# Sparse layer of a four-layer encoder: q, k and v of the first eight heads in steps of 512 columns over four banks

## The chip, the cores and the metric

The kernel runs on one core of one Trainium2 chip. The metric is the device time of one execution in microseconds (us). Engines: PE is TensorE (matmuls), DVE is VectorE, ACT is ScalarE, POOL is GpSimd, SP issues the loads of weights.

## What is computed

Four residual layers, `x <- x + Mixer(RMSNorm(x))`, on 512 tokens of width 1024: a gated short convolution (layer a), sparse attention (layer b), latent attention (layer c), and layer a once more. The change is in layer b:

```python
def dsa_mixer(xn, positions, w_in, q_norm, k_norm, w_out):
    q, k, v, z, qi, ki, wi = jnp.split(xn @ w_in, cuts, axis=-1)
    q = rope(rmsnorm(q.reshape(bsz, seq, B_HEADS, B_HEAD_DIM), q_norm), positions)
    k = rope(rmsnorm(k.reshape(bsz, seq, B_HEADS, B_HEAD_DIM), k_norm), positions)
    ...
        rel = jax.nn.relu(jnp.einsum("qhd,sd->qhs", qi_b, ki_b).astype(jnp.float32))
        score = jnp.einsum("qh,qhs->qs", w_b.astype(jnp.float32), rel)
        ...
        top_val, top_idx = lax.top_k(score, topk)
        ...
        logits = jnp.einsum("qhd,qkhd->qhk", q_b, k_sel).astype(jnp.float32) * scale
    ...
    return (o * jax.nn.silu(z)) @ w_out
```

There are 16 heads of 64, a gate `z` of 1024 columns, and an indexer (`qi`, `ki`, `wi`) whose scores choose 128 keys for each query. Layer b's input projection has 4680 columns.

## The kernel before

Each product of float32 matrices is made of three matmuls, of high and low halves: `products` (lines 277 to 282) multiplies high by high, high by low and low by high into the same PSUM bank. Activations are split once a layer into `xh`, `xl`. Weights come as `raw` tiles of 512 KB from the SP queue, in the order that `enter` (1084 to 1089) writes down, three tiles ahead. `convert` (141 to 163) makes a unit of 512 columns of them: ACT writes the high half `whi` (line 155), POOL the low half `wlo` (line 157). A unit is four rows of eight in a gate block of 128 columns, two in a group of 256 columns, one in a group of 512. Up to three units are made ahead, in rings of four.

Layer b projects first the indexer, then six of its eight gate blocks (`gate_steps`, 712: tile `pz`, 24 matmuls of 512 columns each) and, for heads 0 to 3 (group 0) and 4 to 7 (group 1), q, k and v. `tokens` (311) has the activations of 128 tokens as the stationary side and the weights as the moving one: a group of 256 columns takes 8 x 4 x 3 = 96 matmuls of 256 columns into two banks, each bank holding two blocks of tokens. `project` (866) takes the banks in turn from `pj` and `pt`, two of each. Its finish `fin` (823) runs per bank: ACT copies and squares it (825, 827), DVE sums the squares by head (828), POOL multiplies by the cosine table (`ropea`, line 551), DVE reads the bank twice more for the sine part (`ropeb`, 555), POOL adds (558). Then POOL makes the reciprocal root of the 16 sums per token (`small_rsqrt`, 269, line 274), scales (842 to 851), and `to_features` (563) turns the result with four PE transposes per pair of heads (`tr`), which ACT copies (571) and DVE splits (572).

Beside this `select` (777) makes the index scores: per block of 128 tokens four groups of six matmuls (`si`, line 288), eight `rel` tiles that DVE adds up (792, 794), and 16 rounds of MAX8 and MATCH_REPLACE8 on DVE (799, 800), then a mask (803). Blocks 1, 2 and 3 have 256, 384 and 512 columns; the third mask is `mask3`. `weave` runs the two side by side in the program; the engines' final order is set by a scheduler that works with its own model of times.

`attention` (603) then goes through eight pairs of heads, four blocks of tokens each. The scores of a pair (`s`, line 288) lie in one double bank; DVE adds the mask (638), ACT takes the exponential, DVE the factor `rc` (651), POOL or ACT scales (656, 658), PE turns the probabilities (`pt`, 668). Between these steps a filler runs the projections of groups 2 and 3 (here: late q, k and v), with 256 columns as before and after the change.

Of the kernel before, what the change touches and what calls it, by code (L numbers as in the profile page):

```python
# [10 lines left out]
F32 = mybir.dt.float32  # L11
# [3 lines left out]
OP = mybir.AluOpType  # L15
# [56 lines left out]
def encoder(ctx: ExitStack, tc: tile.TileContext, a, out, depth=4):  # L72
# [6 lines left out]
    def const(shape, name, dtype=F32):  # L79
        return sb.tile(shape, dtype, name=name, bufs=1)  # L80
# [6 lines left out]
    def tile_of(tag, name, shape=(P, S), dtype=F32):  # L87
        return sb.tile(list(shape), dtype, name=name, tag=tag, bufs=BUFS[tag])
# [2 lines left out]
        return tile_of("rp", name, shape, dtype)  # L91

    def tiny(name, n, dtype=F32, tag="tiny"):
        return sb.tile([P, n], dtype, name=name, tag=tag, bufs=24)

    def bank(name, tag):
        return ps.tile([P, S], F32, name=name, tag=tag, bufs=BANKS[tag])
# [132 lines left out]
    def chain(*gens):  # L230
        for g in gens:
            yield from g
# [30 lines left out]
            y = z  # L263
        return y

    minus_half = const([P, 16], "minus_half")
    pool.memset(minus_half, -0.5)

    def small_rsqrt(v, n, scale, out=None):

        m = tiny("mean", n)
# [66 lines left out]
    def by_head(x):  # L338
        return x.rearrange("p (t h) -> p t h", h=4)
# [394 lines left out]
    def layer_b(last):  # L734
# [74 lines left out]
        def token_factors():  # L809

            for name, k in (("r2", None), ("rs", -B_SCALE)):
# [3 lines left out]
                else:  # L815
                    pool.tensor_scalar(st[name], st["r"], k, 0.0, op0=OP.mult, op1=OP.add)


        def query_key(group, which, scales, dst, banks):
            raw = []  # L820
            sums = tiny("hs", 16)

            def fin(i, b):
                x = tile_of("qk", "qk", (P, 2, 256))
                act_e.activation(x.rearrange("p t c -> p (t c)"), b, AF.Copy)
                q = tile_of("rp", "qk2", (P, 2, 256))
# [4 lines left out]
                x5, b5 = (y.rearrange("p t (h i j) -> p t h i j", h=4, i=2)  # L831
                          for y in (x, b.rearrange("p (t c) -> p t c", c=256)))
                C, T = (tab[:, 2 * i:2 * i + 2] for tab in (tq if which == "q" else tk))
                rotate(x5, x5, C, T, b5)

            yield from tokens(group, act, fin, banks)
            v = tiny("hv", 16)
            pool.tensor_tensor(out=by_head(v), in0=by_head(sums), in1=st["r2"][:, :, None].to_broadcast([P, NT, 4]),
                               op=OP.mult)
            y = small_rsqrt(v, 16, 1.0 / 64)  # L840
            if which == "q":
                pool.tensor_tensor(out=scales, in0=by_head(y), in1=st["rs"][:, :, None].to_broadcast([P, NT, 4]),
                                   op=OP.mult)
            else:
                f = tiny("hf", 16)
                pool.tensor_tensor(out=by_head(f), in0=by_head(y), in1=st["r"][:, :, None].to_broadcast([P, NT, 4]),
                                   op=OP.mult)
            for i, x in enumerate(raw):
                if which == "k":
                    x3 = x.rearrange("p t (h d) -> p (t h) d", d=64)  # L850
                    pool.tensor_tensor(out=x3, in0=x3, in1=f[:, 8 * i:8 * i + 8, None].to_broadcast([P, 8, 64]),
                                       op=OP.mult)

            for p in range(2):
                to_features(dst[p], lambda t: raw[t // 2][:, t % 2, p * P:(p + 1) * P], P)

        def values(group, dst, banks):
            def fin(i, b):
                for j in range(2):
                    t = 2 * i + j  # L860
                    act_e.activation(dst[i][:, j], b[:, j * 256:(j + 1) * 256], AF.Copy, scale=st["r"][:, t:t + 1])
            yield from tokens(group, act, fin, banks)

        sets = {}

        def project(g, tags):
            s = sets[g] = dict(qs=sb.tile([P, NT, 4], F32, name="qs", tag="qs", bufs=2))
            for n, w in enumerate("qkv"):
                banks = [bank("p" + w, tags[n % len(tags)]) for _ in range(2)]
                group = a["b_" + w][g]  # L870
                if w == "v":
                    s[w] = [tile_of("v", "v", (P, 2, 256)) for _ in range(2)]
                    yield from values(group, s["v"], banks)
                else:
                    s[w] = [[tile_of("T", w + "T", dtype=F32R) for _ in range(2)] for _ in range(2)]
                    yield from query_key(group, w, s["qs"], s[w], banks)

        def job(pair, after, fill):
            g, i = divmod(pair, 2)

            def scores(outs, t):
# [17 lines left out]
        attention([job(p, p // 2 - 2, ends[p:p + 2]) for p in range(8)],  # L899
                  Filler([project(g, ["pj"]) for g in range(2, 4)] + [gate_steps(a["b_z"][6:], R, gate)]))  # L900
        branch_out(a["b_out"], gate, last)


# [217 lines left out]
def pack(inputs):  # L1121
# [74 lines left out]
```

## Time and profile before

| | us |
|---|---|
| median of three runs | 1062.6 (1060.54 to 1065.26) |
| the profiled execution's own time | 1062.74 |
| its span | 1060.9 |
| PE busy | 1043.6 |
| POOL busy | 694.1 |
| DVE busy | 531.2 |
| ACT busy | 511.2 |

The profile is of one execution; the times in it run from the start of its span. Busy time of an engine is the time in which at least one instruction is on it; matmuls overlap, so PE's busy time says little about how fast they follow one another, for which one looks at their starts. Idle time is shown with what ended it. The first gate block of layer b starts at 254.1 us, layer c at 569.0.

### The profile page before, as it was taken

What the parts mean: (1) busy time and instruction counts of PE and PEld (TensorE: products, weight loads), DVE (VectorE), ACT (ScalarE), POOL (GpSimd) and SP (SyncE); (2) the same over time, 40 slices, a digit from 0 to 9 for tenths busy, and PEclk for the clock granted to TensorE, in tenths of its full rate; (3) what the DMA queues carried; (4) which work ended last, traced back from release to release, by engine and by line L of the source; (5) the groups of instructions that cost most, each with busy time, mean ns of one, the idle gap of its engine ahead of it and who ended that gap; (6) DMA issues with size and microseconds to landing.
All of it is one profiled execution on the core that took longest, in us unless ns stands there. A gap on an engine that the chain in (4) does not pass through costs nothing.

```text
span 1060.9 us, 16208 instructions
## 1 busy us (share of the span) xinstructions
PE 1043.6 (98%) x6040; PEld 877.3 (83%) x6040; DVE 531.2 (50%) x1064; ACT 511.2 (48%) x1082; POOL 694.1 (65%) x637
## 2 busy tenths in 40 slices
PE   8999999999999999999999999999999999999998
PEld 7888888898798999998788777787878888888887
DVE  6784334435598984343535233444542764344321
ACT  6243323433444457666744437876773533333231
POOL 6656555666469799686548689788743855555552
PEclk9999999999999999999999999999999999999999
DMA  6333333323222131111122221101211333333332
GB/s 207 106 114 88 95 97 100 92 69 110 80 80 80 61 99 41 61 61 54 48 70 77 81 74 50 41 23 61 80 40 40 100 99 99 99 100 99 99 100 80
DMA packets 26574, 86.43 MB, mean 81 GB/s; under 512 B 3328, under 2 KB 4096, under 8 KB 26496
## 3 DMA queue, kind: packets, MB, share of 16 engines
q1 hardware_dynamic: 26352, 85.36, 25.6%
q8 instruction: 47, 0.77, 0.3%
q14 instruction: 31, 0.25, 0.1%
q10 hardware_dynamic: 144, 0.05, 0.0%
HBM read 83.30 MB, written 2.10 MB: 80 GB/s over the span
## 4 chain that ended last, share of the span: by engine, by line
PE 91%; POOL 3%; ACT 2%; DVE 2%; issue 1%; DMA 1%; SPq 0%; POOLq 0%; ACTq 0%; DVEq 0%
PE pa L281 11%; PE pa L279 10%; PE pa L280 10%; PE po L279 6%; PE po L280 6%; PE po L281 5%; PE o L689 3%; PE pt L668 3%; PE s L1062 3%; PE pz L281 2%; PE pz L279 2%; PE pz L280 2%; PE s L288 2%; PE tr L568 2%; PE pq L279 2%; PE pk L280 1%
## 5 line engine op out<-in xcount | busy, mean ns | idle before, releaser
L157 POOL TENSOR_TENSOR wlo<-raw,whi 128x512 fp32r<-128x512 f32 (+4 forms) x316 | 408.6, 1300 | 260.3 <-ACT whi L155 256.1
L155 ACT ACTIVATE whi<-raw 128x512 fp32r<-128x512 f32 (+3 forms) x320 | 195.5, 615 | 334.6 <-PE pa L280 157.5
L280 PE MATMUL pa<-xl,whi 128*128 128x512 f32 x512 | 199.4, 389 | 1.1 <-DVE xl L358 1.1
L279 PE MATMUL pa<-xh,whi 128*128 128x512 f32 x512 | 198.9, 390 | 0.2 <-ACT xh L357 0.2
L281 PE MATMUL pa<-xh,wlo 128*128 128x512 f32 x512 | 198.1, 389 | 0.4 <-POOL wlo L157 0.4
L280 PEld LDWEIGHTS pa<-xl,whi 128*128 128x128 f32 x512 | 96.1, 188 | 21.8 <-DVE xl L358 1.7
L279 PEld LDWEIGHTS pa<-xh,whi 128*128 128x128 f32 x512 | 96.3, 188 | 20.6 <-ACT xh L357 0.8
L281 PEld LDWEIGHTS pa<-xh,wlo 128*128 128x128 f32 x512 | 96.0, 188 | 20.9 <-POOL wlo L157 0.9
L656 POOL TENSOR_SCALAR p<-p,rc 128x128 f32<-128x128 f32 (+1 forms) x64 | 69.3, 1088 | 45.5 <-DVE rc L651 45.2
L641 ACT ACTIVATE p<-p,mn 128x128 f32<-128x128 f32 (+3 forms) x128 | 71.0, 557 | 16.5 <-DVE mn L638 16.4
L463 DVE TENSOR_TENSOR cg<-pa,R 128x512 f32<-128x512 f32 x16 | 11.0, 690 | 123.4 <-PE pa L281 121.1
L638 DVE CUSTOM_DVE_ANT_0 p<-s,cmask,qs 128x128 f32<-128x128 f32 (+2 forms) x80 | 37.8, 505 | 35.2 <-PE s L1062 21.2
L281 PE MATMUL pz<-xh,wlo 128*128 128x512 f32 x128 | 51.3, 403 | 0.1
L279 PE MATMUL pz<-xh,whi 128*128 128x512 f32 x128 | 50.9, 398 | 0.2 <-ACT whi L155 0.2
L673 ACT ACTIVATE p<-pt 128x384 f32<-128x384 f32 (+1 forms) x80 | 39.1, 507 | 24.8 <-PE pt L668 24.6
L280 PE MATMUL pz<-xl,whi 128*128 128x512 f32 x128 | 50.4, 394 | 0.0
L280 PE MATMUL po<-xl,whi 128*128 128x512 f32 x128 | 50.3, 393 | 0.0
L668 PE MATMUL pt<-ident,p 128*128 128x128 f32 x320 | 49.2, 277 | 1.0 <-ACT p L673 0.7
L274 POOL TENSOR_TENSOR y<-mean,minus_half 128x16 f32<-128x16 f32 (+1 forms) x18 | 49.6, 2757 | 0.7
L280 PE MATMUL po<-glo,whi 128*128 128x512 f32 x128 | 49.8, 389 | 0.0
L279 PE MATMUL po<-xh,whi 128*128 128x512 f32 x128 | 49.5, 398 | 0.0
L279 PE MATMUL po<-ghi,whi 128*128 128x512 f32 x128 | 49.5, 389 | 0.0
(244 smaller groups left out, 2432.4 us busy)
## 6 DMA issues: line engine op xcount, KB each, us to landing
raw<-in_a_in SPq DMA_DIRECT2D x63, 512.0 KB, 3.9
raw<-in_a_out SPq DMA_DIRECT2D x16, 512.0 KB, 3.9
raw<-in_b_z SPq DMA_DIRECT2D x8, 512.0 KB, 3.5
raw<-in_b_q SPq DMA_DIRECT2D x8, 512.0 KB, 3.5
raw<-in_b_k SPq DMA_DIRECT2D x8, 512.0 KB, 3.5
raw<-in_b_v SPq DMA_DIRECT2D x8, 512.0 KB, 3.5
raw<-in_b_out SPq DMA_DIRECT2D x8, 512.0 KB, 3.9
raw<-in_c_z SPq DMA_DIRECT2D x8, 512.0 KB, 3.5
```

The lines of the kernel that those rows point to most:

```text
L155: act_e.activation(hi[:, :, :n], raw[:, j:j + m], AF.Copy)
L157: e.tensor_tensor(out=lo, in0=raw[:, j:j + m, :n - few], in1=hi[:, :, :n - few].bitcast(F32), op=OP.subtract)
L274: pool.tensor_tensor(out=y, in0=m, in1=minus_half[:, :n], op=OP.pow)
L279: nc.tensor.matmul(o, l[0], r[0], start=first, stop=False)
L280: nc.tensor.matmul(o, l[0], r[1], start=False, stop=False)
L281: nc.tensor.matmul(o, l[1], r[0], start=False, stop=last)
L638: dve.tensor_tensor_reduce(out=p[:, w], in0=banks[e][:, w], in1=j["masks"](t), scale=j["qs"](e, t), scalar=-GONE, op0=OP.add, op1=OP.min, ...
L641: act_e.activation(p[:, w], p[:, w], AF.Exp, bias=mn[e][:, i:i + 1], scale=-1.0, accum_out=sm[:, e * n + i:e * n + i + 1])
L656: pool.tensor_scalar(p[:, w], p[:, w], rc[:, i:i + 1], None, op0=OP.mult)
L668: pe.transpose(b[:, i:i + P], p[:, i:i + P], ident)
L673: act_e.activation(p[:, :n], b[:, :n], AF.Copy)
L689: pe.matmul(o[64 * e:64 * e + 64, t * P:(t + 1) * P], j["v"](e, kb), x[e][:, i:i + P], start=first, stop=t == 0)
```

## The change

The weights of q, k and v for heads 0 to 7 are stored as one group of 512 columns each. `tokens` takes such a group with 8 x 4 x 3 = 96 matmuls of 512 columns into four banks, one block of tokens in each; the four are the two of `pj` and the two of `pt`, for q, for k and for v alike. The early part of layer b becomes: gate blocks 0, 1, 2, q, gate block 3, k, gate block 4, v, gate block 5. Blocks 3 to 5 use the bank `o`, so the transposes from there on have only `tr`. One reciprocal root covers 32 columns in place of two of 16, in place. The ring of small tiles has 20 buffers for 24. Groups 2 and 3 are as they were.

```diff
-    minus_half = const([P, 16], "minus_half")
+    minus_half = const([P, 32], "minus_half")
...
         def query_key(group, which, scales, dst, banks):
+
+            heads = group.n // 64
+            per = NT // len(banks)
             raw = []
-            sums = tiny("hs", 16)
+            sums = sb.tile([P, NT * heads], F32, name="hs", tag=f"hs{heads}", bufs=2)
 
             def fin(i, b):
-                x = tile_of("qk", "qk", (P, 2, 256))
+                x = tile_of("qk", "qk", (P, per, group.n))
                 act_e.activation(x.rearrange("p t c -> p (t c)"), b, AF.Copy)
...
             yield from tokens(group, act, fin, banks)
...
+            y = by_token(sums, heads)
+            pool.tensor_tensor(out=y, in0=y, in1=st["r2"][:, :, None].to_broadcast([P, NT, heads]), op=OP.mult)
+            small_rsqrt(sums, NT * heads, 1.0 / 64, sums)
...
-            for p in range(2):
-                to_features(dst[p], lambda t: raw[t // 2][:, t % 2, p * P:(p + 1) * P], P)
+            for p, x in enumerate(dst):
+                to_features(x, lambda t: raw[t // per][:, t % per, p * P:(p + 1) * P], P)
...
+        def only_tr():
+            early_turns[0] = False
+            yield from ()
...
-        early = chain(gate_steps(a["b_z"][:4], R, gate, "pj"), project(0, ["pj", "pt"]),
-                      gate_steps(a["b_z"][4:6], R, gate, "pj"), project(1, ["pj", "pt"]))
+        def four(name):
+            return lambda: [bank(name, tag) for tag in ("pj", "pj", "pt", "pt")]
+
+        early = chain(gate_steps(a["b_z"][:3], R, gate, "pj"), only_tr(),
+                      *(x for i, which in enumerate("qkv") for x in
+                        (project(which, [0, 1], four("p" + which)), gate_steps(a["b_z"][3 + i:4 + i], R, gate, "o"))))
...
-            enter(a["b_idx"] + a["b_z"][:4])
-            for g in range(4):
+            enter(a["b_idx"] + a["b_z"][:3])
+            for i, w in enumerate("qkv"):
+                enter([a["b_" + w][0], a["b_z"][3 + i]])
+            for g in range(1, 3):
                 enter([a["b_" + w][g] for w in "qkv"])
-                if g == 0:
-                    enter(a["b_z"][4:6])
             enter(a["b_z"][6:] + a["b_out"])
...
-        groups["b_" + n] = [put(f"b_{n}_{i}", w, slice(c + 256 * i, c + 256 * i + 256)) for i in range(4)]
+        groups["b_" + n] = [put(f"b_{n}_{i}", w, slice(c + d, c + e))
+                            for i, (d, e) in enumerate(((0, 512), (512, 768), (768, 1024)))]
```

Three places of the engines' order, before and after. First POOL (`wlo` are low halves of weights, `ropea` and `qk` rotary products and sums, `y` or `hs` with `minus_half` the root). Before, at the root of group 1's q:

```order
L838 TENSOR_TENSOR hv_3485<-hs_3320,br2_2322 128x16
L272 TENSOR_SCALAR mean_3487<-hv_3485 128x16
L274 TENSOR_TENSOR y_3489<-mean_3487,minus_half_94 128x16
L551 TENSOR_TENSOR ropea_3652<-qk_3647,table_1860 128x512
L551 TENSOR_TENSOR ropea_3663<-qk_3658,table_1860 128x512
L157 TENSOR_TENSOR wlo_3734<-raw_3697,whi_3733 128x512
L842 TENSOR_TENSOR qs_3313<-y_3489,brs_2324 128x16
L157 TENSOR_TENSOR wlo_3764<-raw_3761,whi_3763 128x512
L558 TENSOR_TENSOR qk_3647<-ropea_3652,ropeb_3654 128x512
```

Now, at the root of k:

```order
L551 TENSOR_TENSOR ropea_3186<-qk_3181,table_1860 128x512
L558 TENSOR_TENSOR qk_3170<-ropea_3175,ropeb_3177 128x512
L844 TENSOR_TENSOR hs_2946<-hs_2946,br2_2322 128x32
L272 TENSOR_SCALAR hs_2946<-hs_2946 128x32
L558 TENSOR_TENSOR qk_3181<-ropea_3186,ropeb_3188 128x512
L274 TENSOR_TENSOR hs_2946<-hs_2946,minus_half_94 128x32
L157 TENSOR_TENSOR wlo_3346<-raw_3343,whi_3345 128x512
L157 TENSOR_TENSOR wlo_3362<-raw_3343,whi_3361 128x512
L157 TENSOR_TENSOR wlo_3386<-raw_3383,whi_3385 128x512
```

The root now has twice the columns, stands right behind the rotary sum of k's last bank (`qk_3181`), and right behind it comes the low half of v's fifth slice, `wlo_3346`; before, two rotary products stood between a root and the next low half.

Second DVE, at the end of the scoring (`ISA` with a mask among its inputs is the masked addition of line 638, `m8` and `score` are of the scoring rounds). Before:

```order
L799 MAX m8_3829<-score_3260 128x8
L800 MATCH_REPLACE score_3260<-m8_3829,score_3260 128x512
L799 MAX m8_3832<-score_3260 128x8
L828 TENSOR_REDUCE hs_3869<-qk2_4043 128x8
L555 TENSOR_TENSOR ropeb_4048<-pq_3863,table_1855 128x8x32 x2
L800 MATCH_REPLACE score_3260<-m8_3832,score_3260 128x512
L828 TENSOR_REDUCE hs_3869<-qk2_4054 128x8
L555 TENSOR_TENSOR ropeb_4059<-pq_3864,table_1855 128x8x32 x2
L572 TENSOR_TENSOR kT_3509<-tr_3679,kT_3508 128x512
L803 TENSOR_SCALAR mask3_2321<-score_3260 128x512
L572 TENSOR_TENSOR kT_3511<-tr_3686,kT_3510 128x512
L638 ISA p_3990,mn_3992<-s_3983,mask3_2321,qs_2609 128x512
```

Now:

```order
L799 MAX m8_3521<-score_3101 128x8
L638 ISA p_3629,mn_3631<-s_3621,mask2_2320,qs_2326 128x384
L638 ISA mn_3631 128x1
L800 MATCH_REPLACE score_3101<-m8_3521,score_3101 128x512
L572 TENSOR_TENSOR kT_2941<-tr_3221,kT_2940 128x512
L803 TENSOR_SCALAR mask3_2321<-score_3101 128x512
L651 RECIPROCAL rc_3669<-sum_3632 128x2
L638 ISA p_3679,mn_3681<-s_3672,mask3_2321,qs_2326 128x512
L638 ISA mn_3681 128x1
L638 ISA p_3680,mn_3682<-s_3672,mask3_2321,qs_2326 128x512
```

Before, late q's sums and sine products (`pq`) stood ahead of the third mask, and the factor `rc` of the block of 384 columns still further ahead; now they come behind the mask, and that factor, `rc_3669`, stands right behind it.

Third PE, from the transposes behind late q in the kernel before, and, in the changed one, from the scores that need the third mask to the next scores:

```order
L279 MATMUL pq<-whi,xh 128x256
L280 MATMUL pq<-wlo,xh 128x256
L281 MATMUL pq<-whi,xl 128x256
L668 MATMUL pt<-ident,p 128x128 x2
L568 MATMUL tr<-ident,qk 128x128 x8
L668 MATMUL pt<-ident,p 128x128 x4
L279 MATMUL pk<-whi,xh 128x256
L280 MATMUL pk<-wlo,xh 128x256
```

Now:

```order
L288 MATMUL s<-kT,qT 128x512 x6
L279 MATMUL pq<-whi,xh 128x256
L280 MATMUL pq<-wlo,xh 128x256
L281 MATMUL pq<-whi,xl 128x256
L279 MATMUL pq<-whi,xh 128x256
L280 MATMUL pq<-wlo,xh 128x256
L281 MATMUL pq<-whi,xl 128x256
L279 MATMUL pq<-whi,xh 128x256
L280 MATMUL pq<-wlo,xh 128x256
L281 MATMUL pq<-whi,xl 128x256
L668 MATMUL pt<-ident,p 128x128 x6
L288 MATMUL s<-kT,qT 128x128 x6
```

Before, the next scores came only after most of late k; now nine products and six transposes of probabilities, three of them of the block scaled with `rc_3669`, lie between the two.

## Rows read from the trace of the kernel before

**Rows 1.** The page: busy time of each engine; the granted clock in 40 slices, tenths
```profile
PE 1043.6 (98%) x6040; PEld 877.3 (83%) x6040; DVE 531.2 (50%) x1064; ACT 511.2 (48%) x1082; POOL 694.1 (65%) x637
...
PEclk9999999999999999999999999999999999999999
```

**Rows 2.** What PE waited for, 254 to 420: total, times, longest (us)
```profile
PE tr L568 <- DVE key L760: 1.8, 2, 1.5
```

**Rows 3.** Stretches: length, busy (count) of PE, PEld, DVE, ACT, POOL, clock, DMA, GB/s
```profile
340.00:375.00 35.00, 35.00 (x288) 33.72 (x288) 34.35 (x76) 15.09 (x27) 27.04 (x22) 1.00 0.22 72
375.00:400.00 25.00, 24.60 (x206) 23.07 (x204) 19.59 (x51) 16.16 (x40) 24.66 (x24) 1.00 0.28 85
400.00:508.00 108.00, 108.00 (x947) 95.82 (x947) 48.45 (x147) 75.99 (x193) 84.12 (x76) 1.00 0.17 55
```

**Rows 4.** The same view, PE first, for one tile: pv narrow, po wide
```profile
312.09:323.70 11.61, 11.61 (x96) 11.47 (x96) 0.61 (x2) 1.00 0.18 59
...
545.69:568.98 23.29, 23.29 (x102) 19.06 (x102) 4.41 (x7) 1.00 0.29 92
```

**Rows 5.** POOL by line and shape, 254 to 420: busy us, mean ns, idle before
```profile
L157 POOL TENSOR_TENSOR wlo<-raw,whi 128x512 fp32r<-128x512 f32 x47 | 62.5, 1334 | 26.9 <-ACT whi L155 26.6
...
L558 POOL TENSOR_TENSOR qk<-ropea,ropeb 128x512 f32<-128x512 f32 x12 | 15.7, 1309 | 3.0 <-DVE score L796 1.6 <-DVE ropeb L555 1.0 <-PE pk L281 0.4
...
L274 POOL TENSOR_TENSOR y<-mean,minus_half 128x16 f32<-128x16 f32 x5 | 14.6, 2912 | 0.3
...
L656 POOL TENSOR_SCALAR p<-p,rc 128x384 f32<-128x384 f32 x2 | 2.5, 1244 | 0.0
```

**Rows 6.** The same for the whole span: the root of four columns
```profile
L274 POOL TENSOR_TENSOR rtok<-mean,minus_half 128x4 f32<-128x4 f32 x2 | 2.1, 1037 | 0.2
```

**Rows 7.** DVE in order of time: start, duration (us), [idle before, releaser]
```profile
293.42 0.43 DVE L799 MAX8 m<-score 128x8 f32<-128x256 f32 x1
...
321.91 0.56 DVE L799 MAX8 m<-score 128x8 f32<-128x384 f32 x1
...
323.16 0.56 DVE L799 MAX8 m<-score 128x8 f32<-128x384 f32 x1
...
325.70 0.49 DVE L792 TENSOR_SCALAR score<-rel,wi 128x512 f32<-128x512 f32 x1 [1.98 <-ACT rel L788]
...
335.81 0.69 DVE L423 SCALAR_TENSOR_TENSOR zr<-pz,R 128x512 f32<-128x512 f32 x1 [2.29 <-PE pz L281]
...
378.99 0.18 DVE L651 RECIPROCAL rc<-sum 128x4 f32<-128x4 f32 x1 [0.87 <-ACT p L641]
...
383.23 0.62 DVE L638 CUSTOM_DVE_ANT_0 p<-s,mask,qs 128x384 f32<-128x384 f32 x1 [2.68 <-PE s L288]
...
394.75 1.57 DVE L803 TENSOR_SCALAR mask<-score 128x512 f32<-128x512 f32 x1
```

**Rows 8.** DVE by line and shape, 293 to 400
```profile
L828 DVE TENSOR_REDUCE hs<-qk 128x8 f32<-128x512 f32 x10 | 6.4, 673 | 0.0
...
L794 DVE SCALAR_TENSOR_TENSOR score<-rel,wi,score 128x512 f32<-128x512 f32 x7 | 6.3, 904 | 0.0
...
L555 DVE TENSOR_TENSOR ropeb<-pk,table 128x256 f32<-128x256 f32 x8 | 3.0, 411 | 0.0
...
L572 DVE TENSOR_TENSOR kT<-tr,kT 128x512 fp32r<-128x512 f32 x4 | 2.6, 677 | 0.0
...
L426 DVE SCALAR_TENSOR_TENSOR gate<-th,zr 128x512 f32<-128x512 f32 x2 | 2.0, 1025 | 0.2 <-ACT th L425 0.2
```

**Rows 9.** PE in order of time: two groups of index products
```profile
291.05 0.62 PE L288 MATMUL si<-kiT,iT 64*128 64x256 f32 x6
...
335.70 0.97 PE L288 MATMUL si<-kiT,iT 64*128 64x512 f32 x6
```

**Rows 10.** PE in order of time: the first product behind late q
```profile
392.46 0.36 PE L279 MATMUL pk<-whi,xh 128*128 128x256 f32 x1 [0.40 <-ACT qk L827]
```

**Rows 11.** PE in order of time: the first wide products of the kernel
```profile
5.59 1.40 PE L279 MATMUL pa<-xh,whi 128*128 128x512 f32 x3
```

More of the change, by code (lines that the diff above doesn't have):

```diff
@@ L93, in tiny @@
     def tiny(name, n, dtype=F32, tag="tiny"):
-        return sb.tile([P, n], dtype, name=name, tag=tag, bufs=24)
+        return sb.tile([P, n], dtype, name=name, tag=tag, bufs=20)
     def bank(name, tag):
@@ L264, in rsqrt @@
         return y
-    minus_half = const([P, 16], "minus_half")
+    minus_half = const([P, 32], "minus_half")
     pool.memset(minus_half, -0.5)
     def small_rsqrt(v, n, scale, out=None):
-        m = tiny("mean", n)
+        m = tiny("mean", n) if out is not v else v
         pool.tensor_scalar(m, v, scale, EPS, op0=OP.mult, op1=OP.add)
@@ L830, in fin @@
                 raw.append(x)
-                x5, b5 = (y.rearrange("p t (h i j) -> p t h i j", h=4, i=2)
-                          for y in (x, b.rearrange("p (t c) -> p t c", c=256)))
-                C, T = (tab[:, 2 * i:2 * i + 2] for tab in (tq if which == "q" else tk))
+                x5, b5 = (y.rearrange("p t (h i j) -> p t h i j", h=heads, i=2)
+                          for y in (x, b.rearrange("p (t c) -> p t c", c=group.n)))
+                C, T = (tab[:, per * i:per * i + per] for tab in (tq if which == "q" else tk))
                 rotate(x5, x5, C, T, b5)
             yield from tokens(group, act, fin, banks)
[L837 to L840, printed above, removed]
+            y = by_token(sums, heads)
+            pool.tensor_tensor(out=y, in0=y, in1=st["r2"][:, :, None].to_broadcast([P, NT, heads]), op=OP.mult)
+            small_rsqrt(sums, NT * heads, 1.0 / 64, sums)
             if which == "q":
-                pool.tensor_tensor(out=scales, in0=by_head(y), in1=st["rs"][:, :, None].to_broadcast([P, NT, 4]),
-                                   op=OP.mult)
-            else:
-                f = tiny("hf", 16)
-                pool.tensor_tensor(out=by_head(f), in0=by_head(y), in1=st["r"][:, :, None].to_broadcast([P, NT, 4]),
-                                   op=OP.mult)
+                for g, x in enumerate(scales):
+                    pool.tensor_tensor(out=x, in0=y[:, :, 4 * g:4 * g + 4],
+                                       in1=st["rs"][:, :, None].to_broadcast([P, NT, 4]), op=OP.mult)
+            else:
+                pool.tensor_tensor(out=y, in0=y, in1=st["r"][:, :, None].to_broadcast([P, NT, heads]), op=OP.mult)
             for i, x in enumerate(raw):
@@ L857, in values @@
         def values(group, dst, banks):
+            per = NT // len(banks)
             def fin(i, b):
-                for j in range(2):
-                    t = 2 * i + j
-                    act_e.activation(dst[i][:, j], b[:, j * 256:(j + 1) * 256], AF.Copy, scale=st["r"][:, t:t + 1])
+                for j in range(per):
+                    t = per * i + j
+                    for g in range(len(dst) // 2):
+                        c = j * group.n + g * 256
+                        act_e.activation(dst[2 * g + t // 2][:, t % 2], b[:, c:c + 256], AF.Copy,
+                                         scale=st["r"][:, t:t + 1])
@@ L862, in values, with new_set @@
             yield from tokens(group, act, fin, banks)
         sets = {}
[L866 to L876, printed above, removed]
+        def new_set(g):
+            sets[g] = dict(qs=sb.tile([P, NT, 4], F32, name="qs", tag="qs", bufs=2))
@@ new lines, in project @@
+        def project(which, gs, banks):
+            group = a["b_" + which][0 if len(gs) > 1 else gs[0] - 1]
+            if which == "v":
+                dst = []
+                for g in gs:
+                    sets[g]["v"] = [tile_of("v", "v", (P, 2, 256)) for _ in range(2)]
+                    dst += sets[g]["v"]
+                yield from values(group, dst, banks())
+            else:
+                dst = []
+                for g in gs:
+                    sets[g][which] = [[tile_of("T", which + "T", dtype=F32R) for _ in range(2)] for _ in range(2)]
+                    dst += sets[g][which]
+                yield from query_key(group, which, [sets[g]["qs"] for g in gs], dst, banks())
@@ L878, in job, with late @@
+        def late(g):
+            new_set(g)
+            for which in "qkv":
+                yield from project(which, [g], lambda: [bank("p" + which, "pj") for _ in range(2)])
         def job(pair, after, fill):
@@ L899, in layer_b @@
         attention([job(p, p // 2 - 2, ends[p:p + 2]) for p in range(8)],
-                  Filler([project(g, ["pj"]) for g in range(2, 4)] + [gate_steps(a["b_z"][6:], R, gate)]))
+                  Filler([late(g) for g in range(2, 4)] + [gate_steps(a["b_z"][6:], R, gate)]))
         branch_out(a["b_out"], gate, last)
```

8 lines of the change are left out of this document (6 added, 2 removed).

## Prediction

> **What bounds the kernel now.** I read the page's busy table first: TensorE (PE) is busy 98% of the span, every other engine 65% or less, and its granted clock stands at full speed in all 40 slices [rows 1]. That share counts overlapped matmuls, so I read next who made PE wait, in the 166 us from the first gate block on: two waits of 1.8 us together, for the indexer's keys, and hardly anything else [rows 2]. PE works there without a gap, and a matmul less is time less, unless a wait comes in its place. So I looked for engines with little room: DVE is busy 34.35 of 35 us from 340 to 375, and POOL 24.66 of 25 from 375 to 400 [rows 3]. DVE runs the top-k scoring (`select`) there, POOL the low halves of the weights and the rotary products. Each works through its queue in the order in which it stands, so these two are the ones to follow.
>
> **The matmuls.** The change turns 576 matmuls of 256 columns (two groups, q, k and v, 96 each) into 288 of 512. An undisturbed run of 96 narrow ones takes 11.61 us, 0.1209 each; of 102 wide ones 23.29 us, 0.2283 each [rows 4]. 576 x 0.1209 = 69.6 us become 288 x 0.2283 = 65.8: **-3.9 us** on PE. Transposes, index products, gate products and all later ones stay as many. Splitting some transposes into single ones (four of q's, four of k's) costs PE under 0.1 us each, covered by the rounding here.
>
> **The same work elsewhere.** Copies, squares, sums and rotary products are per bank, eight banks before and after, and weigh the same. Four reciprocal roots of 128x16 on POOL become two of 128x32. No row shows that shape; 128x16 takes 2.91 us and 128x4 1.04 [rows 5, 6]. Bounds: 2.9 (as long as 16 columns) and 5.8 (two of them). I take 5.4, by the slope (2.91 - 1.04)/12 = 0.156 us a column. The SP queue issues as many loads of 512 KB in another order, each with three buffers ahead as before: nothing, as POOL's conversion, not a landing, is what frees them. The larger `minus_half` and the ring of 20 tiny tiles cost nothing: a fill at the start, and a ring used in turn by one engine.
>
> **From q to k.** After q's last product POOL has eight rotary steps of 1.3 us and the root of 5.4, 16 us in all [rows 5]. But the order puts k's first two low halves ahead of or between them, and PE has a gate block (24 x 0.228 = 5.5 us) and each wide slice (12 x 0.228 = 2.7 us) against 1.33 us for its low half. I find no wait: the four banks are evacuated bank by bank, and PE's order takes k's first slices in that way too.
>
> **From k to v.** Call k's last product K. By the order DVE has, from the subtract for q's third pair of heads to the rotary product of k's last bank: six scoring rounds at 1.25 us (from one MAX8 of 384 to the next), four score additions of 0.9, four sums of 0.67, eight rotary products of 0.41, two subtracts of 0.68, the gate's two steps, 0.69 and 1.03, and one of 0.49 [rows 7, 8]: 20 us, less the overlap of some 0.07 that starts show, 18.5. I start it at K - 1 (the transposes it needs stand 12 matmuls ahead of K, so K - 2.7 at best). Then POOL: last rotary sum 1.3, root 5.4, and behind it the low half of v's fifth slice, 1.33 [rows 5]: K - 1 + 18.5 + 8.1 = K + 25.6. PE until it needs that: gate 5.5, 48 + 4 wide products of v 11.9, three index groups 2.7 (0.9 each, [rows 9]), transposes 0.4: K + 20.5. **A wait of 5.1 us**, part of it for banks. At worst two roots' worth later, 8; at best none.
>
> Here the rows of the order meet a rule. They show v's products entering bank by bank (two slices into bank 0, then three into bank 1, and so on), so that a late fourth bank delays only the fourth part. The Trainium skill ("Perfetto Trace Analysis", Optimizing Tensor Performance) asks that independent groups rotate through different banks, so that one's evacuation overlaps the next one's matmuls; q, k and v now share four banks. If v had to wait for all four, it would begin at K + 17.5 where the gate ends at K + 6.8, a wait of 10.7 in place of the 5.1, and the sum below would be +6.4 instead of +2.6.
>
> **DVE's chain.** Attention cannot pass its first full block before the third mask (128x512), the end of the scoring: the probabilities' factor, POOL's 1.24 us of scaling for 384 columns and three transposes stand behind the mask in DVE's order and ahead of the next scores in PE's. In the kernel before, scoring ran from the first MAX8 at 293.42 to the mask's end at 394.75 + 1.57 = 396.3: 102.9 us, of which DVE idled 1.98 + 2.29 + 0.87 + 2.68 = 7.8 [rows 7]. 95.1 us of work. PE did not feel it, because the order has 69 matmuls of late q and k and 19 transposes between the scores that need the mask and the next ones. In the change's order it lies otherwise:
> - the first index group keeps its place, the fourth now has 65 wide products ahead of it instead of 17 wide and 59 narrow ones: 14.8 us against 11.0. It starts at 291.05 + 3.8, the first MAX8 at 297.2 [rows 7, 9];
> - ahead of the mask the late q's two sums and four rotary products go (3.0), one gate block's two steps and one subtract come (1.7 + 0.7): 94.5 us.
> Mask at 391.7 without idling. Of the 7.8 us idle I keep 1.5: DVE is 4 us later against PE, which eats most of its waits for PE; bounds 0 and 7.8. Then 0.15 + 1.24 + 0.33 + hand-offs 0.2 = 1.9: the next scores start at **395.1**.
>
> **The sum.** Just ahead of those scores the change has issued the same set of matmuls that the kernel before had finished at 392.5 (q, k and v of both groups, six gates, late q, 52 transposes, nine of the probabilities) [rows 10]. PE's own way there: 392.5 - 3.9 - 0.4 (a wait of the old order [rows 10]) + 5.1 = 393.3. DVE's way: 395.1. The later one counts: 395.1 - 392.5 = **+2.6 us**. Behind that point both orders do equal work, with PE full and DVE at 48 of 108 us [rows 3], and soon run word for word alike, so nothing is won or lost. The profiled execution took 1062.74 us (span 1060.9), 0.1 above the median of 1062.6: 1065.3, **1065 us**.
>
> **Rivals.**
> - A, the forecast: the saving is taken back by the scoring chain and, beside it, v's weights. 1061 to 1068.
> - B, the saving stays: the scoring chain has 48 rounds with small gaps between dependent steps (about 0.05 us at 96 places) that evacuation work may fill, 4.8 us. Without idling DVE's way is then 391.7 - 4.8 + 1.9 = 388.8, and if v's weights come in time PE's is 388.2: 388.8 - 392.5 = -3.7, 1059.0. For it: these gaps are in the rows, and the order was made with them. Against it: the old order filled them too and still took 102.9 us.
> - C, slower: PE and DVE wait for one another after k. DVE's subtract of k's first transposes stands in its queue among the scoring rounds, and those transposes stand in PE's queue behind v's fifth slice. While PE's wait there is under 5.1 + (395.1 - 393.3) = 6.9 us it hides beside the chain; beyond that the mask itself comes later, one for one. With DVE idling 7.8 as before the scores start at 401.4, +8.9 or 1071.6; with a wait of 10.5 us in place of 5.1, +6.2 or 1068.9. A wait of v for all four banks, as above, comes to 1069 too; the order speaks against it, and its chance is counted here. For C: POOL had next to no room from 375 on even before.
> - D, a clock that falls in the wait at v. No row shows it: through the longest wait here, 1.5 us, the clock stayed at full speed [rows 1, 2]. The first three wide products of the kernel took 1.40 us, 0.47 each, twice the 0.228 [rows 11]; one slice of twelve at that rate costs 2.9 us more, PE's way 396.2, +3.7 or 1066.4. The Trainium skill ("TensorE: Matmul & The Clock Gate", HAM oscillation) says that an idle TensorE drops from 2.4 to 1.2 GHz and recovers only under work; the trace so far has no wait long enough to bear it out.
> - That the change doesn't widen anything is out: the order shows 288 products of 512.
>
> **How the numbers follow.** A 0.50, B 0.20, C 0.23, D 0.07. From 0.5% up or down (5.3 us, about what a measurement of this kernel tells from no change) the time counts as changed: below 1057.3 only B's lower end with run-to-run spread, 0.06; above 1067.9 most of C and a corner of A, 0.20; between, 0.74. The range takes A, B and D whole and C up to 1070.5, from 1059.
>
> **What would show it.** In the new profile: wide products at 0.228 us; PE waiting for `wlo` on POOL in v, behind a root of some 5.4 us, or for DVE's evacuation there; the 512-column mask near 393, later than PE; PE waiting ahead of the second pair's first scores for POOL's scaling or DVE. No such waits and a mask before 389: B. A mask past 397 with DVE idle for PE: C. A granted clock under 1.00 after v: D. The forecast is wrong if the wait lies elsewhere, or the mask comes early and the time is still unchanged.

## The result, and the profile after

The changed kernel takes 1070.59 us (median of 6 runs, 1069.86 to 1072.62), the kernel before 1062.23 in the same series: a ratio of 1.0081, interval 1.0069 to 1.0094. It is **slower by 8.4 us**. The forecast was 1065.0 with a range up to 1070.5 and a chance of 0.20 for slower: the time lies just outside, on the side of the rival C. One execution in the whole series, 1152.22 us at a granted clock of 0.851 (e9_dve_root_noscore below), was slow, and the ratios leave it out.

The page first: busy times, and the granted clock in 40 slices.

```profile
PE 1043.9 (98%) x5752; PEld 862.8 (81%) x5752; DVE 531.6 (50%) x1064; ACT 511.8 (48%) x1082; POOL 694.4 (65%) x630
...
PEclk9999999999999899999999999999999999999999
```

The totals are nearly those of [rows 1], but one slice of the clock has fallen. The waits of PE from 254 to 420 us (total, times, longest), against [rows 2]:

```profile
PE pv L280 <- POOL wlo L157: 5.0, 1, 5.0
PE tr L568 <- DVE key L760: 1.8, 2, 1.5
PE pv L279 <- DVE ropeb L555: 1.7, 2, 1.5
PE pk L279 <- DVE ropeb L555: 0.4, 1, 0.4
```

The second was there before. The first is new and lies in v; of the third, 1.53 us stand ahead of v's first product and 0.22 later in v. The fourth, at 400 us, is as long as the 0.4 us that the kernel before waited there for ACT. The stretches (length, busy and count of PE, PEld, DVE, ACT, POOL, clock, DMA, GB/s) show where the clock was low:

```profile
340.00:362.80 22.80, 16.11 (x70) 11.05 (x68) 22.63 (x50) 8.29 (x15) 19.92 (x14) 0.97 0.08 24
362.80:368.20 5.40, 5.34 (x13) 4.19 (x14) 5.17 (x11) 0.63 (x1) 4.80 (x6) 0.50 0.37 109
368.20:400.00 31.80, 31.52 (x214) 27.23 (x212) 25.50 (x63) 17.79 (x43) 18.95 (x18) 1.00 0.25 81
```

PE in order of time, from the gate block behind k to the scores behind the third mask:

```profile
340.86 0.39 PE L281 MATMUL pz<-xh,wlo 128*128 128x512 f32 x1
342.77 0.47 PE L279 MATMUL pv<-whi,xh 128*128 128x512 f32 x1 [1.53 <-DVE ropeb L555]
...
356.79 1.07 PE L279 MATMUL pv<-whi,xh 128*128 128x512 f32 x4
362.86 0.80 PE L280 MATMUL pv<-wlo,xh 128*128 128x512 f32 x1 [5.00 <-POOL wlo L157]
...
366.44 1.91 PE L279 MATMUL pv<-whi,xh 128*128 128x512 f32 x4
368.15 0.47 PE L280 MATMUL pv<-wlo,xh 128*128 128x512 f32 x1
...
398.02 0.81 PE L668 MATMUL pt<-ident,p 128*128 128x128 f32 x6
398.76 0.95 PE L288 MATMUL s<-kT,qT 64*128 64x128 f32 x12
```

PE waits 1.53 us ahead of v's first product, for DVE's reads of k's banks, and 5.00 us in v's fifth slice, for its low half. Then twelve products take 368.15 - 362.86 = 5.3 us, 0.59 the first and 0.43 each of the others in place of 0.228: at half clock (0.50, the lower level of 1.2 GHz), 2.4 to 2.6 us lost. The Trainium skill ("TensorE: Matmul & The Clock Gate", Back-to-back issue gap) gives columns / 1.2 GHz for a cold array, by which 427 ns is the estimate for 512 columns. The 0.43 us of these rows agree with that. The scores that the forecast put at 395.1 start at 398.76, and PE waits for nothing at that place. What POOL did meanwhile:

```profile
354.31 1.86 POOL L558 TENSOR_TENSOR qk<-ropea,ropeb 128x512 f32<-128x512 f32 x1
356.13 5.44 POOL L274 TENSOR_TENSOR hs<-hs,minus_half 128x32 f32<-128x32 f32 x1
361.54 5.10 POOL L157 TENSOR_TENSOR wlo<-raw,whi 128x512 fp32r<-128x512 f32 x4
...
395.37 1.28 POOL L157 TENSOR_TENSOR wlo<-raw,whi 128x512 fp32r<-128x512 f32 x1 [3.19 <-ACT whi L155]
396.63 1.25 POOL L656 TENSOR_SCALAR p<-p,rc 128x384 f32<-128x384 f32 x1
```

The last rotary sum of k, the root, and then four low halves, for the first of which PE waits; at the end, a low half and the scaling that stand ahead of the transposes at 398.02. And DVE, from the first round to the third mask:

```profile
297.08 0.43 DVE L799 MAX8 m<-score 128x8 f32<-128x256 f32 x1
...
353.08 0.74 DVE L555 TENSOR_TENSOR ropeb<-pk,table 128x256 f32<-128x256 f32 x2
...
379.79 0.69 DVE L572 TENSOR_TENSOR kT<-tr,kT 128x512 fp32r<-128x512 f32 x1 [3.24 <-ACT kT L571]
...
394.81 0.42 DVE L803 TENSOR_SCALAR mask<-score 128x512 f32<-128x512 f32 x1
```

Between these times DVE idled 3.24 us for k's transposes, which stand behind v on PE, and 0.6 elsewhere.

### The profile page after: what moved, and what is told of

Read it like the earlier page. It is cut to its first block, busy times and chain, and to the rows that moved or that the text cites. A ratio compares the mean times of both kernels' runs of the same rounds, so it can differ in the third digit from the quotient of the medians.

```text
span 1068.7 us, 15612 instructions
## 1 busy us (share of the span) xinstructions
PE 1043.9 (98%) x5752; PEld 862.8 (81%) x5752; DVE 531.6 (50%) x1064; ACT 511.8 (48%) x1082; POOL 694.4 (65%) x630
## 4 chain that ended last, share of the span: by engine, by line
PE 90%; POOL 3%; DVE 3%; issue 2%; ACT 2%; DMA 1%; SPq 0%; POOLq 0%; ACTq 0%; DVEq 0%
PE pa L279 11%; PE pa L281 11%; PE pa L280 11%; PE po L279 5%; PE po L280 5%; PE po L281 5%; PE o L689 3%; PE pt L668 3%; PE s L1096 3%; PE pz L281 2%; PE pz L279 2%; PE pz L280 2%; PE s L288 2%; PE tr L568 2%; PE pk L281 1%
## 5 line engine op out<-in xcount | busy, mean ns | idle before, releaser
L281 PE MATMUL po<-xh,wlo 128*128 128x512 f32 x128 | 48.6, 393 | 0.0
```

Of the source, the lines that this page charges most:

```text
L281: nc.tensor.matmul(o, l[1], r[0], start=False, stop=last)
```

## The experiments

All times are medians in us; the ratio is to the kernel before, in runs beside it.

| run | us | ratio | interval |
|---|---|---|---|
| e1_no_root | 1069.32 | 1.0065 | 1.0049 to 1.0082 |
| e2_short3 | 1070.03 | 1.0073 | 1.0058 to 1.0088 |
| e4_half | 1071.00 | 1.0079 | 1.0064 to 1.0094 |
| e5_g2121 | 1067.24 | 1.0047 | 1.0029 to 1.0065 |
| e6_short2 | 1069.97 | 1.0069 | 1.0044 to 1.0094 |
| e7_dummy | 1068.03 | 1.0050 | 1.0033 to 1.0067 |
| e8_before_noscore | 1062.28 | 0.9998 | 0.9987 to 1.0009 |
| e8_after_noscore | 1066.24 | 1.0036 | 1.0025 to 1.0048 |
| e9_dve_root | 1074.76 | 1.0110 | 1.0095 to 1.0125 |
| e9_dve_root_noscore | 1060.05 | 0.9974 | 0.9964 to 0.9983 |
| e9_dve_root_g2121 | 1071.24 | 1.0089 | 1.0071 to 1.0106 |
| e10_behind | 1073.10 | 1.0097 | 1.0080 to 1.0114 |
| e11_w_none | 1064.33 | 1.0014 | 1.0004 to 1.0023 |
| e11_w_k | 1068.36 | 1.0057 | 1.0041 to 1.0073 |
| e11_w_qv | 1065.91 | 1.0034 | 1.0022 to 1.0047 |
| e11_w_v | 1061.73 | 1.0001 | 0.9991 to 1.0011 |
| e12_v_in_old_places | 1065.03 | 1.0016 | 1.0006 to 1.0026 |
| e12_wv_3021 | 1061.64 | 0.9989 | 0.9978 to 1.0000 |

### Is it the pause, or the scoring chain?

The theory of the record, S here, says that DVE's chain to the third mask sets the time; its rival P says that PE's pause in v does. The first run leaves out k's root.

```diff
-            small_rsqrt(sums, NT * heads, 1.0 / 64, sums)
+            if which == "k" and heads == 8:
+                pool.tensor_scalar(sums, sums, 1.0 / 64, EPS, op0=OP.mult, op1=OP.add)
+            else:
+                small_rsqrt(sums, NT * heads, 1.0 / 64, sums)
```

> k's 32 sums per token get the scaled mean only; the power (5.44 us on POOL) is left out, so k is scaled wrongly. Theory P (the pause of PE in v is the loss: 5.0 us for the fifth slice's low half behind the root, and the clock's fall behind it, 2.4 us): the pause and the fall go, the 1.5 us for the bank at v's start stays, 1070.6 - 7.4 = 1063 to 1064.5. Theory S (the scoring chain of DVE sets the time and PE's pause lies beside it): pause gone, but the third mask still ends near 395 and the time stays above 1067.

Measured 1069.32, above 1067 as S had it, but the pauses did not go, which neither had expected. POOL of this run, in order of time:

```profile
353.73 1.86 POOL L558 TENSOR_TENSOR qk<-ropea,ropeb 128x512 f32<-128x512 f32 x1
355.55 0.23 POOL L854 TENSOR_TENSOR hs<-hs,rtok 128x32 f32<-128x32 f32 x1
355.86 4.94 POOL L858 TENSOR_TENSOR qk<-qk,hs 128x512 f32<-128x512 f32 x4
360.77 2.50 POOL L157 TENSOR_TENSOR wlo<-raw,whi 128x512 fp32r<-128x512 f32 x2
```

The scaling of k, 4.94 us, moved into the root's place, so the low halves start 0.8 us earlier and no more; PE still waits there, 2.6 us ahead of k's transposes, which now stand within v, 1.8 for DVE's reads and 0.8 for a low half, 5.1 in all (6.8 in the change), and the clock still fell. The run decides nothing between P and S; what it shows is that POOL's queue holds v's weights, whichever long instruction stands in it.

The second run takes half of the rounds from the third block, which follows k's evacuation.

```diff
-                for r in range(TOPK // 8):
+                for r in range(TOPK // 8 if t < 3 else TOPK // 16):
```

> The third block of index scores gets 8 rounds of MAX8 and MATCH_REPLACE8 instead of 16, so its mask is another one; 8 x 1.52 = 12 us less of DVE work ahead of the third mask, all of it behind k's evacuation. P: pause (5.0), the clock's fall and the time stay, 1069.5 to 1071.5. S: the mask comes some 10 us sooner and the time falls by 3.5 or more, to 1067 or less.

Measured 1070.03: S falls. The third mask starts at 373.48, 21 us earlier, yet the next scores start at 398.84, where the change has 398.76, behind the same wait:

```profile
PE pv L280 <- POOL wlo L157: 5.0, 1, 5.0
```

Splitting the root lets a low half in between:

```diff
-            pool.tensor_tensor(out=y, in0=y, in1=st["r2"]...)
-            small_rsqrt(sums, NT * heads, 1.0 / 64, sums)
+            for t in range(0, NT, 2):
+                ...
+                pool.tensor_tensor(out=v, in0=v, in1=minus_half[:, :16], op=OP.pow)
```

> Each root of 32 columns is made as two of 16, by halves of the tokens; in POOL's order one low half of v (the fifth slice's) now stands ahead of the second. P: the pause of 5.0 falls to under 1.5, the clock stays at full speed, 1063 to 1065. S: above 1067 whatever becomes of the pause.

Measured 1071.00. The wait for the low half fell to 0.5, but the scheduler's new order puts DVE's first read of k's banks at 348.47 (341.88 in the change), behind more scoring, and PE waits as long at v's beginning:

```profile
349.36 0.76 PE L279 MATMUL pv<-whi,xh 128*128 128x512 f32 x1 [6.39 <-DVE ropeb L555]
```

The clock fell there as well, within that wait. So the pause has a second source, DVE's reads.

More of PE's work between k and v covers both:

```diff
-        early = chain(gate_steps(a["b_z"][:3], ...), only_tr(), ... gate_steps(a["b_z"][3 + i:4 + i], ...)
+        cuts = [2, 3, 5, 6]
+        early = chain(gate_steps(a["b_z"][:cuts[0]], ...), only_tr(), ... gate_steps(a["b_z"][cuts[i]:cuts[i + 1]], ...)
```

> Gate blocks 2, 1, 2, 1 instead of 3, 1, 1, 1: one block moves from ahead of q to between k and v, 24 wide products or 5.5 us more for POOL and DVE to finish k. P: no pause over 1 us in v, nor at its start, no fall of the clock, 1061 to 1064. S: the pause goes, but the time stays above 1067.

Measured 1067.24, 3.4 less than the change, 3 more than P hoped. The big pause is gone; in its place there are several:

```profile
PE pv L279 <- DVE ropeb L555: 2.3, 2, 2.1
...
PE pk L279 <- DVE ropeb L555: 1.7, 1, 1.7
PE s L288 <- DVE mn L638: 1.6, 1, 1.6
PE pv L280 <- POOL wlo L157: 0.8, 1, 0.8
```

With PE no longer late, the scores wait for DVE: S's chain is the next bound, not the present one. The clock did not stay up, as P had it: it fell at 397 us, behind the two waits of 1.6 us (scores) and 1.7 us (late k).

### DVE or POOL?

P2 puts the pause down to DVE's rounds, Q to POOL or the banks.

```diff
-                for r in range(TOPK // 8):
+                for r in range(TOPK // 8 if t != 2 else TOPK // 16):
```

> The second block of index scores gets 8 rounds instead of 16 (its mask is another one): 8 x 1.25 = 10 us less of DVE work in the queue ahead of k's evacuation. Theory P2 (DVE, busy with these rounds, reads k's four banks too late; v's first products and, over POOL's sums, root and low half, v's fifth slice wait for that): both pauses in v fall under 1 us, no fall of the clock, 1061 to 1064. Theory Q (four banks used anew with one gate block between are too few at any speed of DVE, or POOL's root is): a pause of over 3 us stays in v and the time over 1067.

Measured 1069.97. The wait at v's beginning fell from 1.5 to 0.7 us, but the one for the low half is 6.0: P2 alone falls. The pair without scoring says it more plainly:

```diff
-                for r in range(TOPK // 8):
+                for r in range(1):
```

> The kernel before with one round for each block of index scores instead of 16 (other masks): DVE has some 60 us less to do. It had no waits of PE to lose there, so the time stays within 2 us of 1062.2.

> The changed kernel with one round for each block, to be held against the one before. P2: with DVE free the four banks are read in time, no pause over 1 us in v, and what the wide products save remains: 2.5 to 3.9 us less than the other. Q: pauses in v stay, and it is 2 us or more slower than the other.

1062.28 and 1066.24. The kernel before is as long with 16 rounds as with one. The changed one keeps a pause, for POOL alone:

```profile
PE pv L280 <- POOL wlo L157: 4.2, 1, 4.2
```

The wait for DVE at v's beginning is gone, so that one was DVE's. Now the root goes to DVE, with nothing to take its place on POOL:

```diff
-            small_rsqrt(sums, NT * heads, 1.0 / 64, sums)
+            dve.tensor_scalar(v, sums, 1.0 / 64, EPS, op0=OP.mult, op1=OP.add)
+            rsqrt(v, ..., out=sums)
```

> The roots of 32 columns are made on DVE, by the shift and three Newton steps that the kernel has for other roots (12 small operations each), and no longer on POOL; in POOL's order nothing comes into their place: v's fifth low half now stands right behind the sums of k's last bank. Theory Q1 (POOL's queue makes the pause: root, 5.44 us, and in the run without it the scaling, 4.94 us, stand ahead of v's fifth low half): the pause of 5.0 falls under 1 us, no fall of the clock, the 1.5 us at v's start stays: 1063 to 1065. Theory P2 (DVE's lateness alone): a pause of 3 us or more stays, over 1067.

> The same with one round for each block of index scores, to be held against the changed kernel with one round (1066.2) and the kernel before with one round (1062.3). Q1: no pause, no fall of the clock: 4.2 + 2.8 us under the former, 1058.5 to 1060, so 2.5 to 3.8 under the latter. If four banks with one gate block between are too few in themselves, a pause for DVE's reads stays and it is not under 1061.

> Roots on DVE and gate blocks 2, 1, 2, 1. Q1 and P2 together (POOL's queue and DVE's reads each have a share): no pause over 1 us in v at all, the third mask near 392 as in the run with 2, 1, 2, 1 alone, and DVE's masks and POOL's scaling the next bound: 1061 to 1064. If it is 1065 or more, DVE's chain, longer by 24 small operations, has taken the gain.

With scoring 1074.76, far over the 1065 that Q1 allowed: no wait for POOL's low halves is left, but DVE's queue is longer, and PE waits 2.2, 2.2, 2.0, 0.9 and 0.9 us in other places: for a high half of ACT, POOL's scaling, and DVE's reads and subtracts. With blocks 2, 1, 2, 1 it takes 1071.24, and PE waits for DVE at v (3.0 us), at transposes, at scores and at late k. Without scoring **1060.05**: no wait in v, and the stretch of the pauses is full, at full clock:

```profile
340.00:375.00 35.00, 35.00 (x177) 28.36 (x176) 21.60 (x44) 16.93 (x37) 28.98 (x24) 1.00 0.27 86
```

Its ratio stands 0.0024 under that of the kernel before without scoring: 2.5 us, with some 1.6 us of noise either way. The executions of both whose mean granted clock was 1.000 differ by 1.5 us (1059.61, five of them, and 1061.12, three), and so do the traces from layer b's first product to layer c (312.8 and 314.3). So 1.5 to 2.5 us is what the wide products bring with these waits gone; the places of the gate blocks and of the roots differ in this pair too. Against the changed kernel without scoring it gains 6.2 us, the wait of 4.2 and the slow products behind it.

The four banks are the same here, and from q to v PE does not wait for one: the rule weighed in the forecast (the Trainium skill, "Perfetto Trace Analysis", Optimizing Tensor Performance: rotate independent groups through banks) does not bite by itself here; it bites where the reader of a bank is busy.

The last of this kind leaves the root on POOL and ties it to v's fifth low half, taken up later in the program:

```diff
+                pool.tensor_scalar(one, ready[0][0][1][:, 0:1].bitcast(F32), 0.0, 1.0 / 64, op0=OP.mult, op1=OP.add)
+                pool.tensor_scalar(sums, sums, one, EPS, op0=OP.mult, op1=OP.add)
```

> Root on POOL as in the change, but bound to v's fifth low half (its scale is read from a tile made from it) and taken up later in the program: POOL makes six low halves first, and k's root, scaling and transposes follow 15 us later. Q1: the pause of 5.0 falls under 1 us and the clock stays; the time then depends on attention's later start: 1063 if nothing waits there, up to 1068 if scores wait for k's transposes.

Measured 1073.10. The wait for the low half is gone, the 1.5 at v's beginning stays, and the clock is full until 380. But k's root, scaling and transposes come later, the scores with them, and PE stands there: 3.3 us for DVE's subtract, at a clock of 0.50 from 390 to 400. Moving the wait saved nothing: the median is 2.5 us above the change's, and the intervals overlap.

### What the clock takes

```diff
+            for i, _ in enumerate(tokens(group, act, fin, banks)):
+                if group.n == 512 and i == 3:
+                    for _ in range(20):
+                        pe.matmul(b, x[:, :P], newest[0][1], start=True, stop=True)
+                yield
```

> 20 matmuls of 512 columns that nobody reads (20 x 0.228 = 4.6 us) go into a bank of their own behind v's fourth slice, into the pause. If the fall of the clock costs what its slow products show (12 x 0.2 = 2.4 us): granted clock 1.00 throughout, pause under 1 us, 1067.5 to 1069. If the fall costs nothing (PE would wait elsewhere instead): 1070 to 1071.

Measured 1068.03, 2.6 less than the change. PE's stretches (length, busy, clock, DMA, GB/s):

```profile
340.00:362.00 22.00, 20.04 (x88) 1.00 0.07 25
362.00:369.00 7.00, 6.49 (x29) 1.00 0.41 137
```

The low half comes when it did, but the clock is full behind it, and layer c starts 320.3 us behind layer b's first product, where the change has 323.3. So the fall costs 2.6 to 3.0 us, about what its slow products show, and PE makes nothing good later.

### Which part of the change

R: wide k makes the pause. Four runs keep the change's places and choose the widths:

```diff
+            if which in WIDE:
+                yield from project(which, [0, 1], four("p" + which))
+            else:
+                for g, tag in enumerate(("pj", "pt")):
+                    yield from project(which, [g], lambda: [bank("p" + which, tag) for _ in range(2)])
```

> The change's places (a gate block behind q, k and v, in the bank o, one tr) with all products of 256 columns again, two groups each, banks pj and pt in turn. Theory R (wide k makes the pause: all of its evacuation, its one root and its scaling come at once, and v's weights stand behind them): no pause over 1 us in v, 1061 to 1064, the kernel before within noise. If the places themselves (gates, one tr) cost: 1066 or more.

> Only k in 512 columns. R: a pause of 3 to 6 us in v with the fall of the clock behind it, 1066 to 1070. If the pause needs all three wide: under 1 us, 1060 to 1063.

> The change with k alone undone (two groups of 256, each with its own root of 16 columns). R: no pause over 1.5 us in v, clock full, two thirds of the saving of 3.5 remain: 1060 to 1063. Otherwise a pause of 3 us or more and over 1066.

> Only v in 512 columns; v has neither a root nor rotary products, its four banks are read by ACT. R: no pause over 1 us, a third of the saving: the run with all narrow less 1.2, 1060 to 1063.

Only k wide has the pause again, and with it the fall of the clock (0.63 from 363 to 367 us):

```profile
PE pv L280 <- POOL wlo L157: 3.9, 1, 3.9
```

It costs 1.0057 - 1.0014 = 0.0043, 4.6 us, over the same places with nothing wide, which themselves cost 1.5 us (1.0014). Wide v alone gains 0.0013, 1.4 us (the intervals overlap), a third of the 3.9 of the forecast, and stands at the time of the kernel before. Wide q and v without wide k have no pause in v, but 1.6, 1.2 and 0.9 us of waits for DVE at scores and transposes, and 1.0034, where R had hoped for at most 1063. That is 0.0033, 3.5 us, over wide v alone, with the intervals apart: wide k makes the pause, but wide q has a price as well, through DVE. Wide q by itself was not run. Two more places for wide v, in words, against e11_w_v:

```text
-        early = chain(gates 0 to 2, q, gate 3, k, gate 4, wide v, gate 5)
+        early = chain(gates 0 to 3, q and k of group 0, gate 4, q and k of group 1, gate 5, wide v)
```

> The kernel before with v of heads 0 to 7 alone as 96 products of 512 columns (192 narrow ones less, 96 wide ones more): q and k per group in 256, gate blocks 0 to 3 ahead of them, 4 and 5 behind the groups, v last. By R nothing of POOL's or DVE's stands in v's way that did not before: 1062.4 less 1.2, 1060.5 to 1062. If v's later start hurts (attention begins without the gate block behind v), 1062.5 to 1065.

```text
-        early = chain(gates 0 to 2, q, gate 3, k, gate 4, wide v, gate 5)
+        early = chain(gates 0 to 2, q, k, gates 3 and 4, wide v, gate 5)
```

> Only v wide, as e11_w_v, with the gate block between q and k moved to between k and v (3, 0, 2, 1). R: no pause in v, 1060 to 1062; if q's evacuation needs the gate block behind it, waits of k for DVE come and it is over 1063.

The first lost 1.7 us on the kernel before, with a wait of 2.2 us ahead of k's transposes for DVE; the second gained 1.2 (0.9989) with an interval that ends at 1.0000. It beats the change by 9 us; that it beats the kernel before is not settled: among the executions with a mean granted clock of 1.000 it took 1060.95 us (four), the kernel before 1061.20 (nine).

## Why the prediction was right or wrong

- **What bounds.** Right: PE has no slack, DVE and POOL have little, and both came up.
- **The matmuls, -3.9.** Right in rate, too big in sum. Counting each early product from its start to PE's next start, the 576 narrow ones took 71.5 us (forecast 69.6) and the 288 wide ones 77.0, of which 8.1 are the pauses inside v and the half clock: 68.9 (forecast 65.8). So 2.6 us: the wide runs are cut by transposes and index groups too, and a product ahead of or behind such a cut takes up to 0.34 us. In the free pair the same count gives 71.6 and 68.7.
- **The root.** 5.4 by the slope, 5.44 measured. **q to k:** no wait, as forecast.
- **k to v.** Right in size and place. Forecast 5.1 us for the fifth low half behind the root, measured 5.00, in that place. Both ends came 3 us later than worked out (K is 334.08 here, where k's products end and the gate block begins: 362.86 is K + 28.8, forecast K + 25.6), DVE's last read at K + 19.7 in place of 17.5. Not seen: 1.5 us at v's beginning. The forecast found v's products entering bank by bank and counted the first bank as free in time; ACT had squared it by 337.52, but DVE read it only at 341.88, behind more scoring (MAX8 at 338.32, 339.57 and 340.82).
- **The clock.** This is the step that failed most. The fall stood apart as rival D, at 0.07, and at nothing in the sum, while the forecast itself held a wait three times as long as any in the trace [rows 2] and priced it at its length alone. The fall came, at 2.4 to 2.6 us (D priced it at 2.9), and e7 has 2.6 to 3.0 for it.
- **DVE's chain.** Its work was right: from 297.08 (forecast 297.2) to 395.23 with 3.9 us idle is 94.3 us, forecast 94.5. Its idling was not: 3.9 where 1.5 was taken, 3.24 of it for k's transposes behind v. That is rival C's hold of PE and DVE on each other. Behind the mask POOL took a low half first, and its scaling ended at 397.88, not 1.9 us but 3.5 us from the mask's end to the scores.
- **"The later one counts: 395.1."** The wrong way was chosen. PE's way sets the time: 392.5 - 2.6 - 0.4 + 1.7 + 5.0 + 2.4 = 398.6, measured 398.76, where the forecast had 393.3; the terms are the forecast's own end, the smaller saving, the old wait, the two kinds of wait and the clock. (Layer b began 0.5 us sooner in this execution, so 0.7 us stay without a name.) e2 shows it: a mask 21 us earlier, the same scores at the same time. DVE's way came out nearly level, with POOL's scaling done 0.14 us before PE's transposes of its result, so it is the next bound, as in e5.
- **Nothing won or lost behind that point.** From 392.46 to 398.76 are 6.3 us, and the span grew by 7.8. Wrong by the difference: behind it PE waits 2.0 us in the change up to layer c, 0.6 + 0.5 + 0.5 + 0.4, where the kernel before waits 0.7, which is 1.3 of the 1.5; the rest was not followed up.

So the mechanism that the forecast had for v's weights was right, and its sum for PE's way was not: the clock at nothing, the saving 1.3 us too large, the 1.7 us for DVE's reads left out. The time came within a hair of the range's end, but by terms that the range did not rest on. Rival B is out; the outcome joins A's wait, D's clock and C's hold, which set no time here (e2). The causes are shown by runs that take them away: POOL's queue and DVE's rounds together (e9_dve_root_noscore against e8_after_noscore and e9_dve_root), the clock (e7), wide k as the source of the pause (e11). That wide q costs through DVE's queue is read from its waits and not taken apart.

## What to carry to other kernels

When a forecast contains a wait longer than any in the trace, price what such a wait brings with it, the engine's clock first, in the forecast and not as a rival. Joining groups makes their after-work come at once: ask what stands behind that burst in each queue that it passes, and expect that taking one piece out of a full queue lets the next take its place, as the scaling did here. Only taking away both holds at once let the wider products' gain show.

## What the runs showed of the hardware that was not expected

The clock does not follow the length of a pause alone. In e9_dve_root PE stood 2.03 us at 322.9 and the clock fell; it stood 2.2 us between 370 and 375 and the clock held (PE: length, busy, clock, DMA, GB/s):

```profile
318.00:322.60 4.60, 4.60 (x24) 1.00 0.34 110
322.60:326.00 3.40, 1.37 (x8) 0.89 0.00 0
326.00:329.50 3.50, 3.50 (x11) 0.62 0.48 150
370.00:375.00 5.00, 2.84 (x13) 1.00 0.00 0
375.00:380.00 5.00, 5.00 (x31) 1.00 0.02 3
```

A closer pair lies ahead of layer c's scores, where PE stands 1.53 us in every trace, for the same subtract of DVE. Behind it the clock held in thirteen of the twenty traces, the kernel before and the changed one among them, and fell in seven. The kernel before, then e11_w_none:

```profile
791.80:795.20 3.40, 3.00 (x15) 1.00 0.00 0
792.70:796.00 3.30, 3.30 (x13) 0.69 0.00 0
```

The kernel's own spread goes with this clock. In the last series the executions of the kernel before with a mean granted clock of 1.000 took 1061.20 us on average (nine), those with 0.998 1063.14 (eight), those with 0.997 1064.71 (five).

The Trainium skill ("TensorE: Matmul & The Clock Gate", HAM oscillation) tells how waits between bursts of matmuls drop the clock, burst after burst. That one pause of the same length and place can end either way is this case's own.

And the third mask, the same instruction on the same shape, took 1.57 us before [rows 7] and 0.42 now. Before, POOL had begun a rotary sum 0.05 us ahead of it, and the mask ended 0.33 us behind that sum; now POOL was idle until 395.37. The kernel before:

```profile
394.70 1.29 POOL L558 TENSOR_TENSOR qk<-ropea,ropeb 128x512 f32<-128x512 f32 x1
```

The same mask in e6_short2, then in e8_after_noscore:

```profile
381.41 1.50 DVE L803 TENSOR_SCALAR mask<-score 128x512 f32<-128x512 f32 x1
353.12 0.43 DVE L803 TENSOR_SCALAR mask<-score 128x512 f32<-128x512 f32 x1
```

The Trainium skill ("SBUF — State Buffer", Who interferes with whom) says that such an operation of VectorE and one of GpSimd hold a shared pair of ports in turn, each for a whole instruction; the two times agree with that. So do other traces: in e6_short2 the third mask began 0.07 us behind a low half of POOL and ended 0.28 us behind it, and in e4_half (1.44 us) and e5_g2121 (1.40 us) it was the same. But not every operation of POOL holds the mask up: in e8_after_noscore it lay wholly beside a root, begun 1.57 us ahead of it, and took 0.43. There the measurement differs from "a whole instruction".
